# Start addresses of the large operands of a two-layer encoder moved to multiples of 64 bytes

## The chip, the cores and the metric

The kernel runs on one core of one Trainium2 chip. What is measured is the device time of one execution in microseconds (us), and the median of several runs is compared. Within the core, TensorE multiplies matrices (PE in the profile; PEld is its loading of the stationary operand), VectorE (DVE) and ScalarE (ACT) work elementwise, GpSimd (POOL) does small extra work, and SyncE (SP) issues most transfers. The operands of all of them lie in an on-chip memory of 128 partitions. A tile takes the same range of bytes in every partition, so that its place is one number: the byte in a partition at which it starts.

## The reference

The reference is an encoder of two layers over 256 tokens with 2048 channels, all in float32. Layer 0 mixes the tokens by gated linear attention in chunks, layer 1 by grouped attention with rotary positions. After each mixer stand an MLP with squared ReLU (2048 to 8192 to 2048) and a gated embedding:

```python
def reference(x, p, ...):
    h = x
    for i in range(DEPTH):                       # 2 layers
        u = rms_norm(h, g_pre_mix[i])
        mix = gla_mixer(u, ...) if i % 2 == 0 else gqa_mixer(u, ...)
        h = h + rms_norm(mix, g_post_mix[i])
        m = squared_relu_mlp(rms_norm(h, g_pre_mlp[i]), w_mlp_up[i], w_mlp_down[i])
        h = h + rms_norm(m, g_post_mlp[i])
        gate = sigmoid(h @ w_ple_gate[i])
        e = p[i] @ w_ple_proj[i]
        h = h + rms_norm(gate * e, g_ple[i])
    return h
```

Most of the arithmetic is products of a 256 x 2048 (or 256 x 8192) activation with weight matrices that are read once.

## The kernel before

Every large product is computed to nearly float32 accuracy from three products in the type float32r: an operand is split exactly into a high and a low part, and high x high, high x low and low x high are summed in one accumulator. The split activation lies in a tile `[128, 16, 512]` of 32 KiB in each partition: 16 contraction tiles of 128 rows, each with 256 columns of high and 256 columns of low part. There are two such tiles, `X` (the normalised residual) and `H` (what a mixer or the first half of the MLP has made).

The weights come through `WeightStream` (line 58), chunk by chunk in the order of use. A chunk is two contraction tiles of 512 columns, 4 KiB in a partition. It is loaded from memory into a `raw` buffer by SyncE (line 82), ACT writes its high part `whi` (line 91), and DVE writes its low part `wlo` (line 92). There are four buffers of each kind.

Two functions multiply:

- `gemm_b` (line 355) has the weights stationary and the activation moving. For each contraction tile and each 128 weight columns it issues a pair: `whi` against all 512 columns of `X` (line 367), then `wlo` against the 256 high columns (line 372). It makes q, k and og of layer 0 and, in four quarters per layer, the upward half of the MLP (u0 to u3; the page calls them all `u`).
- `gemm_a` (line 277) has the activation stationary and the weights moving, three products of 512 columns for each contraction tile and 128 rows (lines 294 to 296). With `X` stationary it makes v of layer 0, the keys, values and queries of layer 1 (kp, vp, q) and the gates (g); with `H` stationary the outputs of the mixers (go, ao) and the downward half of the MLP (d0 to d3).

`gemm_out` (line 301) is `gemm_a` for go, ao, d3 and g. Its last 512 columns are taken one row tile after the other (lines 333 to 335), and the first half of their weights waits in whichever of `X` and `H` is free: `X` for go, ao and d3, `H` for g. So there the moving operand is first one of the two large tiles and then a weight buffer, over the same stationary tile. The first row tile is multiplied 512 columns wide (48 matmuls), the second in two halves of 256.

The page names the moving operand first: `d<-whi,H` is `whi` moving over stationary `H`, `u<-X,whi` is `X` moving over stationary `whi`. The order of PE is the order in which the program is written; DVE and ACT are ordered by a scheduler.

Tiles get their addresses in the order in which pools and tiles are opened: first `ident`, `cols`, `mhalf` and `ones`, then `h` and `X`, then the weight buffers, then the pool `sm` of small tiles, the pool `mem` (tags `m2` and `e4`), and last what is opened for a while: the pool of the linear attention (`core`), or `L1` with `H` as its first tile. Each tile takes a multiple of 32 bytes.

Of the kernel before, what the change touches and what calls it, by code (L numbers as in the profile page):

```python
# [10 lines left out]
F32 = mybir.dt.float32  # L11
# [6 lines left out]
P = 128  # L18
# [17 lines left out]
NCOL = 84  # L36
# [19 lines left out]


class WeightStream:
    """Weight chunks in the order of use: DMA in, split exactly into two float32r parts."""

    def __init__(self, nc, pool, nraw, nsplit):
        self.nc, self.pool, self.nraw, self.nsplit = nc, pool, nraw, nsplit
# [29 lines left out]
        self.todo.append(lambda: self.nc.vector.tensor_sub(lo, raw, hi.bitcast(F32)))  # L92

    def parts(self, i):
        """The first chunk comes one contraction tile at a time, so that PE starts early."""
        kt = self.chunks[i][1]
        return [(k, k + 1) for k in range(kt)] if i == 0 else [(0, kt)]

# [52 lines left out]
def kernel(ctx, tc, a, out):  # L151
    nc = tc.nc
    base = ctx.enter_context(tc.tile_pool(name="base", bufs=1))
# [7 lines left out]
    def acc(name):  # L161
        return psa.tile([P, 512], F32, tag="acc", name=name)
# [60 lines left out]

    ident = base.tile([P, P], F32, name="ident")
    make_identity(nc, ident)
    cols = base.tile([P, NCOL], F32, name="cols")
    mhalf = base.tile([P, 8], F32, name="mhalf")
    nc.gpsimd.memset(mhalf, -0.5)
    ones = base.tile([P, 1], F32, name="ones")
    nc.gpsimd.memset(ones, 1.0)  # L230
    h = base.tile([P, NT, D], F32, name="h")
    X = base.tile([P, KT, 512], F32R, name="X")
# [41 lines left out]
    def region_open():  # L274
        region.enter_context(tc.manual_schedule(engines={mybir.EngineType.Activation, mybir.EngineType.DVE}))

    def gemm_a(op, ngroups, evac, nk=16, name="a", pair=False):
        nch = nk // KC
        order = [(g, c) for g in range(ngroups) for c in range(nch)]
        if pair:  # L280
            order = pair_order(nch) + [(g, c) for g in range(2, ngroups) for c in range(nch)]
        ps = {}
        for g, c in order:
            if c == 0:
                ps[g] = [acc(f"{name}_{g}_{t}") for t in range(NT)]
            hi, lo = W.get()
            seq = [(k, t) for k in range(KC) for t in range(NT)]
            if c == nch - 1:
                seq = [(k, t) for t in range(NT) for k in range(KC)]
            for k, t in seq:  # L290
                K = c * KC + k
                xh = op[:, K, t * P:(t + 1) * P]
                xl = op[:, K, T + t * P:T + (t + 1) * P]
                mm(ps[g][t], xh, hi[:, k], start=K == 0, stop=False)  # L294
                mm(ps[g][t], xh, lo[:, k], start=False, stop=False)  # L295
                mm(ps[g][t], xl, hi[:, k], start=False, stop=K == nk - 1)  # L296
                if K == nk - 1:
                    evac(g, t, ps[g][t])
            yield (g, c)

    def gemm_out(op, keep, evac, name, pair=False):
        """Four column groups; the last one row tile after the other, half of its weights waiting in `keep`."""
        nch = KT // KC
        p0 = W.pos + 3 * nch
        for c in range(NSPLIT):
            W.dest[p0 + c] = [keep[:, 4 * c + 2 * z:4 * c + 2 * z + 2].rearrange("p k n -> p (k n)") for z in range(2)]
        yield from gemm_a(op, 3, evac, name=name, pair=pair)
        for t in range(NT):
            parts = [(0, 512)] if t == 0 else [(0, 256), (256, 256)]
            ps = [acc(f"{name}_3_{t}_{o}") for o, _ in parts]  # L310
            order = [[c] for c in range(nch)]
            if t:
                order = order[NSPLIT:] + order[:NSPLIT]
                order[-2:] = [order[-2] + order[-1]]
            for n, cs in enumerate(order):
                end = n == len(order) - 1
                if t and end:
                    region_open()
                wt = {}
                for c in cs:  # L320
                    W.ahead()
                    wt[c] = W.pop(p0 + c) if t else W.split[p0 + c]
                if t and end:
                    W.pos += nch
                for (o, w), p_ in zip(parts, ps):
                    s = slice(o, o + w)
                    ck = [(c, k) for c in cs for k in range(KC)]
                    for c, k in ck:
                        K = c * KC + k
                        hi, lo = wt[c]  # L330
                        xh = op[:, K, t * P:(t + 1) * P]
                        xl = op[:, K, T + t * P:T + (t + 1) * P]
                        mm(p_[:, :w], xh, hi[:, k, s], start=n == 0 and k == 0, stop=False)
                        mm(p_[:, :w], xh, lo[:, k, s], start=False, stop=False)
                        mm(p_[:, :w], xl, hi[:, k, s], start=False, stop=end and (c, k) == ck[-1])
                    if end:
                        evac(3, t, p_[:, :w], o, w)
                yield (3, cs[0])
# [8 lines left out]
        return r  # L347

    def early(m, ss, name):
        """The update of the residual's first rows, while PE is at the second."""  # L350
        r = rstd_of(ss[:, :1, :4], D, name)
        for n in range(4):
            residual_n(m, r, n, (0,))
# [42 lines left out]
    def at(plan, slot, *fs):  # L396
        plan.setdefault(slot, []).extend(fs)
# [40 lines left out]
                                           op0=ALU.mult, op1=ALU.add)  # L438

    def boundary(m, ss, gain0, name, fill=(), late=None):  # L440
        """The normalised update of the residual and the next operand; fill: products that keep PE busy."""
        rstd = last_rstd(ss, name)
        mults = list(pend)
        pend.clear()
        W.ahead(1, lows=False)
        for f in fill[:-1]:
            f()()
        for o in (0, 256):
            nc.vector.scalar_tensor_tensor(h[:, 1, o:o + 256], m(1, 0)[:, o:o + 256], rstd, h[:, 1, o:o + 256],
                                           op0=ALU.mult, op1=ALU.add)  # L450
        W.lows()
        make_X(0, gain0)
        if late is not None:
            late(0)
        if fill:
            fill[-1]()()
        residual_n(m, rstd, 1, (1,))
        W.ahead(1)

        def hook(n):  # L460
            def f():
                make_X(n, gain0)
                if n == 2:
                    for g in mults:
                        g()
                if n < 3:
                    residual_n(m, rstd, n + 1, (1,))
                if late is not None:
                    late(n)
                if n == 3:  # L470
                    region.close()
            return f
        hooks = {0: [hook(1)], 2: [hook(2)], 4: [hook(3)]}
        if late is not None:
            at(hooks, 6, lambda: late(4))
        return hooks
# [137 lines left out]
    with tc.tile_pool(name="core", bufs=1) as cp:  # L614
# [150 lines left out]
        s = fold(ps, "lr", 32)  # L765
# [35 lines left out]
        sl = drive(gemm_a(X, 4, v_evac, name="v"), plan, sl)  # L801

    L1 = ctx.enter_context(tc.tile_pool(name="L1", bufs=1))
    H = L1.tile([P, KT, 512], F32R, name="H")

    def load_PT(i):
        pts = L1.tile([P, 2, T], F32, tag="pts", name=f"pts{i}")
        nc.scalar.dma_start(pts, a["pT"][i])
        PT = L1.tile([P, 2, 512], F32R, tag="PT", name=f"PT{i}")
        split_into(PT[:, :, :T], PT[:, :, T:], pts)  # L810
        return PT

    def og_evac(i, ps):
        s = fold(ps, f"og{i}")
        t1 = L1.tile([P, T], F32, tag="t1", name=f"og1_{i}", bufs=2)
        nc.vector.tensor_mul(t1, s, R0["r"])
        sg = L1.tile([P, T], F32, tag="t2", name=f"og2_{i}", bufs=2)
        nc.scalar.activation(sg, t1, AF.Sigmoid)
        nc.vector.tensor_mul(t1, t1, on[i // 4][:, i % 4])
        nc.vector.tensor_mul(t1, t1, sg)  # L820
        split_into(H[:, i, :T], H[:, i, T:], t1)
    drive(gemm_b(X, 4, og_evac, name="og"), plan, sl)
# [3 lines left out]
    mg = {}  # L826
    gr = gain_row(L1, a["g_post_mix"][0], "gpm0")
    ss = sm.tile([P, NT, 5], F32, tag="ss", name="ssm0")
    drive(gemm_out(H, X, out_evac(mg, gr, ss, "go"), "go"))

    RM = {}
# [13 lines left out]
    def mlp_ple(i, hooks, PT):  # L845
# [5 lines left out]
        def up_evac(f, ps):  # L851
# [3 lines left out]
            nc.scalar.activation(s2, s, AF.Square)  # L855
            split_into(H[:, f, :T], H[:, f, T:], s2)

# [16 lines left out]
        for q in range(4):  # L874
# [3 lines left out]
            if q < 3:  # L878
                drive(gemm_a(H, 4, down_evac(q), name=f"d{q}"))
            else:  # L880
                drive(gemm_out(H, X, down_evac(q), f"d{q}"))
        hooks = boundary(lambda t, n: macc[t][n], ss, None, f"rpl{i}", eprojs(e, range(EU[0] if i == 0 else EU[2], 8), PT))
        gr2 = {}

# [22 lines left out]
        def upd(t, n):  # L907
            return e[n][:, t]
        drive(gemm_out(X, H, gate_evac, f"g{i}"), hooks)
        return upd, ss2  # L910

# [265 lines left out]
```

## Time and profile before

| | before |
|---|---|
| median of 3 runs | 2332.02 us (2331.41 to 2332.15) |
| span of the profiled execution, first to last instruction | 2329.9 us |
| what lies around the span, median less span | 2.1 us |
| matmuls on PE | 11924 |
| PE busy | 2305.6 us, 99% |
| DVE, ACT busy | 1423.1 us (61%), 1213.8 us (52%) |
[...]

The profiled execution is known by its span alone; a run's time is 2.1 us longer than that span by the median. Matmuls overlap in the profile: each is shown from its own start to the modelled end of its pipeline, so that the next one starts while it is still shown. A busy share of 99% therefore tells that PE never waited long. It does not tell at what pace it went. The pace of a stage is read from the starts of its matmuls: the time from the start of one to the start of another, divided by how many lie between. [...] In a table by windows, the count in brackets is the number of matmuls shown in the window, and windows of the same length can be compared by it.

### The profile page before, as it was taken

How to read it: one execution, taken by the hardware profiler on the slowest of the kernel's cores; microseconds unless marked ns; L12 is line 12 of the kernel's file. 1: busy time of each engine (PE TensorE's matmuls, PEld its weight loads, DVE VectorE, ACT ScalarE, POOL GpSimd, SP SyncE). 2: the span in 40 equal slices, each digit the busy share in tenths (PEclk: the TensorE clock that was granted, in tenths of full speed). 3: DMA queues.
4: the chain of work that ended last, by engine and by line, in shares of the span. 5: the costliest groups of instructions: out<-in, count | busy, mean ns of one | idle time of the engine just before them, and what ended most of it. 6: DMA issues, size and time to landing. Idle time of an engine off the chain costs nothing.

```text
span 2329.9 us, 31200 instructions
## 1 busy us (share of the span) xinstructions
PE 2305.6 (99%) x11924; PEld 1955.4 (84%) x11924; DVE 1423.1 (61%) x1920; ACT 1213.8 (52%) x1884; POOL 36.7 (2%) x58
## 2 busy tenths in 40 slices
PE   8989999999999999999999999999999999999998
PEld 7878888988888888888888888888888888888887
DVE  6787765664564565556667676665455455455565
ACT  6666554654453454454456565555454355355454
POOL 0000000000000000000000010000000000000000
PEclk9999999999999999999999999999999999999999
DMA  8544665665665665665565644565565566566654
GB/s 285 158 145 144 203 187 189 192 188 189 189 190 186 187 188 186 188 191 187 194 216 160 181 137 158 200 190 189 186 187 189 187 189 189 187 187 188 210 171 145
DMA packets 223784, 431.75 MB, mean 185 GB/s; under 512 B 15697, under 2 KB 16721, under 8 KB 222865
## 3 DMA queue, kind: packets, MB, share of 16 engines
q1 hardware_dynamic: 221328, 421.23, 58.7%
q10 hardware_dynamic: 2304, 8.52, 1.0%
q8 instruction: 93, 1.52, 0.3%
q14 instruction: 59, 0.48, 0.1%
HBM read 427.60 MB, written 2.10 MB: 184 GB/s over the span
## 4 chain that ended last, share of the span: by engine, by line
PE 96%; DVE 1%; ACT 1%; issue 1%; DMA 0%; POOL 0%; SPq 0%; DVEq 0%; POOLq 0%; ACTq 0%
PE u L367 20%; PE u L372 10%; PE d L296 10%; PE d L294 10%; PE d L295 10%; PE og L367 3%; PE g L295 2%; PE g L294 2%; PE g L296 2%; PE og L372 1%; PE q L294 1%; PE q L296 1%; PE q L295 1%; PE k L367 1%; PE go L296 1%; PE ao L295 1%
## 5 line engine op out<-in xcount | busy, mean ns | idle before, releaser
L92 DVE TENSOR_TENSOR wlo<-raw,whi 128x1024 fp32r<-128x1024 f32 (+1 forms) x770 | 937.6, 1221 | 751.4 <-ACT whi L91 749.1
L91 ACT CAST whi<-raw 128x1024 fp32r<-128x1024 f32 (+1 forms) x770 | 805.5, 1049 | 875.3 <-PE d L296 357.3
L367 PE MATMUL u<-X,whi 128*128 128x512 f32 x2048 | 716.7, 395 | 0.0
L372 PE MATMUL u<-X,wlo 128*128 128x256 f32 x2048 | 572.1, 280 | 0.0
L367 PEld LDWEIGHTS u<-X,whi 128*128 128x128 f32 x2048 | 383.8, 187 | 89.5
L372 PEld LDWEIGHTS u<-X,wlo 128*128 128x128 f32 x2048 | 386.1, 189 | 0.4
L296 PE MATMUL d<-whi,H 128*128 128x512 f32 x960 | 380.6, 396 | 0.0
L294 PE MATMUL d<-whi,H 128*128 128x512 f32 x960 | 379.7, 395 | 0.0
L295 PE MATMUL d<-wlo,H 128*128 128x512 f32 x960 | 377.3, 393 | 0.0
L295 PEld LDWEIGHTS d<-wlo,H 128*128 128x128 f32 x960 | 180.2, 188 | 44.5
L296 PEld LDWEIGHTS d<-whi,H 128*128 128x128 f32 x960 | 180.2, 188 | 43.9
L294 PEld LDWEIGHTS d<-whi,H 128*128 128x128 f32 x960 | 180.2, 188 | 42.5
L367 PE MATMUL og<-X,whi 128*128 128x512 f32 x256 | 89.4, 393 | 0.0
L294 PE MATMUL g<-whi,X 128*128 128x512 f32 x192 | 75.2, 392 | 0.0
L295 PE MATMUL g<-wlo,X 128*128 128x512 f32 x192 | 74.7, 389 | 0.0
L296 PE MATMUL g<-whi,X 128*128 128x512 f32 x192 | 74.7, 389 | 0.0
L372 PE MATMUL og<-X,wlo 128*128 128x256 f32 x256 | 71.7, 280 | 0.0
L367 PEld LDWEIGHTS og<-X,whi 128*128 128x128 f32 x256 | 47.9, 187 | 10.5
L409 ACT COPY u_c<-u 128x256 f32<-128x256 f32 x128 | 47.1, 368 | 17.1 <-PE u L372 17.1
L367 PE MATMUL q<-X,whi 128*128 128x512 f32 x128 | 46.2, 411 | 6.1 <-ACT whi L91 5.3
L295 PE MATMUL v<-wlo,X 128*128 128x512 f32 x128 | 50.7, 396 | 0.8 <-DVE wlo L92 0.8
L294 PE MATMUL v<-whi,X 128*128 128x512 f32 x128 | 51.5, 402 | 0.0
(426 smaller groups left out, 2978.4 us busy)
## 6 DMA issues: line engine op xcount, KB each, us to landing
raw<-in_w_mlp_up SPq DMA_DIRECT2D x256, 512.0 KB, 3.7
raw<-in_w_mlp_down SPq DMA_DIRECT2D x256, 512.0 KB, 3.8
raw<-in_gla_w_in SPq DMA_DIRECT2D x95, 512.0 KB, 4.0
raw<-in_w_ple_gate SPq DMA_DIRECT2D x64, 512.0 KB, 4.2
raw<-in_attn_w_in SPq DMA_DIRECT2D x48, 512.0 KB, 4.2
raw<-in_gla_w_out SPq DMA_DIRECT2D x32, 512.0 KB, 4.3
raw<-in_attn_w_out SPq DMA_DIRECT2D x32, 512.0 KB, 4.3
raw<-in_w_ple_proj SPq DMA_DIRECT2D x7, 512.0 KB, 5.2
```

Source lines behind the costliest of these rows:

```text
L91: self.nc.scalar.copy(hi, raw)
L92: self.todo.append(lambda: self.nc.vector.tensor_sub(lo, raw, hi.bitcast(F32)))
L294: mm(ps[g][t], xh, hi[:, k], start=K == 0, stop=False)
L295: mm(ps[g][t], xh, lo[:, k], start=False, stop=False)
L296: mm(ps[g][t], xl, hi[:, k], start=False, stop=K == nk - 1)
L367: mm(ps[f], hi[:, k, f * P:(f + 1) * P], op[:, K, :], start=K == 0, stop=K == 15, skip_group_check=True)
L372: mm(ps[f][:, T:], lo[:, k, f * P:(f + 1) * P], op[:, K, :T], start=False, stop=K == 15, skip_group_check=True)
L409: nc.scalar.copy(cr[:parts], ps[:parts, T:])
```

## The change

Three small tiles at the start are made larger, and an unused tile of 32 bytes is put before `H`. The kernel uses the same parts of the enlarged tiles as before. Four docstrings and a class docstring become blank lines, and from the new tile on the lines are one higher.

```diff
-    cols = base.tile([P, NCOL], F32, name="cols")
-    mhalf = base.tile([P, 8], F32, name="mhalf")
+    cols = base.tile([P, 96], F32, name="cols")[:, :NCOL]
+    mhalf = base.tile([P, 16], F32, name="mhalf")[:, :8]
     nc.gpsimd.memset(mhalf, -0.5)
-    ones = base.tile([P, 1], F32, name="ones")
+    ones = base.tile([P, 16], F32, name="ones")[:, :1]
     nc.gpsimd.memset(ones, 1.0)
     h = base.tile([P, NT, D], F32, name="h")
     X = base.tile([P, KT, 512], F32R, name="X")
...
     L1 = ctx.enter_context(tc.tile_pool(name="L1", bufs=1))
+    L1.tile([P, 8], F32, name="gap")
     H = L1.tile([P, KT, 512], F32R, name="H")
```

On every engine the instructions are the same and stand in the same order. What moves is where the tiles start. Below is the first byte of each in a partition, by the built programs, and its remainder by 64. All offsets of the large operands within their tiles are multiples of 512 bytes, so the remainder of the tile is that of the operand.

| tile | before | remainder | after | remainder |
|---|---|---|---|---|
| h | 17440 | 32 | 17536 | 0 |
| X | 33824 | 32 | 33920 | 0 |
| raw (first of four) | 66592 | 32 | 66688 | 0 |
| whi (first of four) | 82976 | 32 | 83072 | 0 |
| wlo (first of four) | 99360 | 32 | 99456 | 0 |
| m2 tiles (first of eight) | 135104 | 0 | 135200 | 32 |
| e4 tiles (first of five) | 151488 | 0 | 151584 | 32 |
| H | 171968 | 0 | 172096 | 0 |
| PT, and the low parts of k and v in layer 1 (in L1) | 210880, 214976 | 0 | 211008, 215104 | 0 |

`X`, `raw`, `whi` and `wlo` move by 96 bytes together, `H` by 128. In layer 0 the operands of the linear attention (v in m2, S in the pool core) go from remainder 0 to 32 together. In layer 1, q, k, v and the softmax in m2 and e4 go from 0 to 32, but the low parts of k and v stay at 0.

## Rows read from the trace of the kernel before

**Rows 1.** The page, parts 1 and 2: busy time by engine; granted clock.

```profile
PE 2305.6 (99%) x11924; PEld 1955.4 (84%) x11924; DVE 1423.1 (61%) x1920; ACT 1213.8 (52%) x1884; POOL 36.7 (2%) x58
...
PEclk9999999999999999999999999999999999999999
```

**Rows 2.** PE's longest wait: who, for whom, us in total, times, longest.

```profile
PE q L367 <- ACT whi L91: 5.3, 1, 5.3
```

**Rows 3.** Windows (us), PE alone: length, busy (matmuls), clock, DMA share, GB/s.

```profile
260.00:320.00 60.00, 60.00 (x348) 1.00 0.64 191
620.00:690.00 70.00, 70.00 (x406) 1.00 0.64 190
700.00:770.00 70.00, 70.00 (x302) 1.00 0.59 188
790.00:860.00 70.00, 70.00 (x397) 1.00 0.64 187
1170.00:1210.00 40.00, 40.00 (x178) 1.00 0.62 207
1700.00:1770.00 70.00, 70.00 (x397) 1.00 0.64 186
1880.00:1950.00 70.00, 70.00 (x406) 1.00 0.66 192
```

**Rows 4.** PE's timeline in d1 of layer 0: start, length shown (us), instruction.

```profile
709.70 0.40 PE L296 MATMUL d<-whi,H 128*128 128x512 f32 x1
...
712.50 0.40 PE L296 MATMUL d<-whi,H 128*128 128x512 f32 x1
```

**Rows 5.** The same in the gate of layer 0.

```profile
1179.80 0.39 PE L296 MATMUL g<-whi,X 128*128 128x512 f32 x1
...
1182.52 0.39 PE L296 MATMUL g<-whi,X 128*128 128x512 f32 x1
```

**Rows 6.** The same at the end of layer 1's gate, from `H` to `whi`.

```profile
2298.71 0.40 PE L333 MATMUL g<-H,X 128*128 128x512 f32 x1
...
2304.56 0.39 PE L334 MATMUL g<-wlo,X 128*128 128x512 f32 x1
...
2306.60 0.39 PE L334 MATMUL g<-wlo,X 128*128 128x512 f32 x1
```

**Rows 7.** The page, part 5: two of the groups over stationary `H`, by line.

```profile
L294 PE MATMUL d<-whi,H 128*128 128x512 f32 x960 | 379.7, 395 | 0.0
...
L294 PE MATMUL go<-whi,H 128*128 128x512 f32 x96 | 37.6, 392 | 0.0
```

**Rows 8.** PE's timeline in u1 of layer 0.

```profile
629.68 0.39 PE L367 MATMUL u<-X,whi 128*128 128x512 f32 x1
...
631.76 0.39 PE L367 MATMUL u<-X,whi 128*128 128x512 f32 x1
```

**Rows 9.** PE's timeline in u2 of layer 0.

```profile
799.70 0.40 PE L367 MATMUL u<-X,whi 128*128 128x512 f32 x1
...
803.94 0.40 PE L367 MATMUL u<-X,whi 128*128 128x512 f32 x1
```

**Rows 10.** PE's timeline at the end of layer 0's gate, 256 columns wide.

```profile
1227.72 0.28 PE L334 MATMUL g<-wlo,X 128*128 128x256 f32 x1
...
1230.84 0.28 PE L333 MATMUL g<-H,X 128*128 128x256 f32 x1
...
1236.12 0.28 PE L333 MATMUL g<-H,X 128*128 128x256 f32 x1
```

**Rows 11.** PE's timeline in the linear attention, 256 columns wide.

```profile
175.35 0.28 PE L732 MATMUL o<-Sh,v 128*128 128x256 f32 x1
...
176.54 0.28 PE L733 MATMUL o<-Sl,v 128*128 128x256 f32 x1
```

**Rows 12.** The page, part 5: the split of the weights on DVE and ACT.

```profile
L92 DVE TENSOR_TENSOR wlo<-raw,whi 128x1024 fp32r<-128x1024 f32 (+1 forms) x770 | 937.6, 1221 | 751.4 <-ACT whi L91 749.1
L91 ACT CAST whi<-raw 128x1024 fp32r<-128x1024 f32 (+1 forms) x770 | 805.5, 1049 | 875.3 <-PE d L296 357.3
```

## The prediction, made before the changed kernel was run

> **What bounds the kernel now.** I read the page's busy times first, then PE's waits, then the starts of its matmuls stage by stage. PE is shown busy for 99% of the span at full clock, and DVE and ACT for 61% and 52% [rows 1]. Its longest wait is 5.3 us, once [rows 2]. So almost all of the 2329.9 us is the pace of PE, and a change that moves no instruction can matter only if it changes that pace.
>
> The pace is not the same everywhere, and that is the finding on which all rests. In the downward MLP (stationary `H`) 12 matmuls of 512 columns take 712.50 - 709.70 = 2.80 us, 233.3 ns each [rows 4]. In the gate (stationary `X`), the same lines with the same weight buffers moving, 12 take 2.72 us, 226.7 ns each [rows 5]. PE waits for nothing in either: both windows are full [rows 3]. [...]
>
> Is that the stage or the operand? At the end of layer 1's gate the stationary tile stays `X`, and the moving operand goes from `H` to the weight buffers. The pace goes from 5.85 us / 25 = 234.0 ns to 2.04 us / 9 = 226.7 ns from the second matmul on [rows 6]. So it depends on the two operands together. `X`, `whi` and `wlo` lie at remainder 32 by 64, `H` at 0. I call a pair of operands alike if both have the same remainder, else unlike. Alike (32 and 32) goes at 226.7 ns; unlike goes at 233.3 (moving 32, stationary 0) and at 234.0 (moving 0, stationary 32).
>
> The pairs of `gemm_b` are alike, and they have two paces at the same addresses: in u1 of layer 0 a pair (512 and 256 columns) takes 2.08 us / 6 = 346.7 ns [rows 8], in u2 4.24 us / 12 = 353.3 ns [rows 9]. By counts u1 of layer 0 and u2 of layer 1 go at the fast pace (406 matmuls in 70 us) and u2 of layer 0 and u1 of layer 1 at the slow one (397); og, which follows v, goes at the fast one (348 in 60 us) [rows 3]. Of the eight upward quarters four are fast and four slow, in turn. A stage keeps the pace that it falls into, so it is the way of entering it that picks one.
>
> **The change part by part.** The enlarged tiles and the gap issue nothing and cost nothing. What they do is move addresses: every large operand gets remainder 0, so that all pairs of `gemm_a` and `gemm_b` are alike.
>
> Stationary `H`: d has 3 x 960 matmuls of 512 columns, go and ao 2 x 3 x 96 [rows 7], which is 3456; the first row tiles of the closings of go, ao and the two d3 add 4 x 48 = 192, and the `H`-moving halves of the two gates 2 x 24 = 48. Together 3696 unlike matmuls. If alike at 0 costs what alike at 32 costs, each saves 233.3 - 226.7 = 6.67 ns: 3696 x 6.67 = **24.6 us**, all of it on the path that sets the end, since PE is that path throughout.
>
> Stationary `X` (v, kp, vp, q, the gates; 1536 + 48 matmuls): alike before and after, 0.
>
> The pairs of `gemm_b` (2560, of which 2048 in the upward quarters, 256 in each): alike before and after. Four quarters are slow: 4 x 256 x 6.67 = 6.8 us can be won if all become fast, or lost if all become slow. All slow quarters are entered from a stage with stationary `H`, which is unlike; og is entered from v, which is alike, and is fast [rows 3]. After the change all are entered from an alike stage, so og is the nearest row, and I take **6.8 us** won. Bounds: 6.8 won to 6.8 lost.
>
> Matmuls of 256 columns outside the pairs are about a thousand: 120.0 ns alike at 32 and 117.3 unlike (the first and the second stretch of [rows 10]), about 119.0 alike at 0 [rows 11]. Some of them become unlike or alike at 32 (layer 1's attention). With 1.0 ns or less between either and the middle, times some thousand, I set 0, bounds 2.7 us either way.
>
> Cover: at 226.7 ns a chunk of 12 matmuls lasts 2.72 us. Its split takes 1.05 us on ACT and 1.22 us on DVE [rows 12], so both have over half of it in hand, and the gate already runs full at this pace with its transfers at 207 GB/s [rows 3]. Nothing new becomes late. Elementwise tiles that go from 0 to 32 join `raw`, `whi` and `wlo`, which are worked on at 32 now; none of this work is what PE waits for, so I set it at 0.
>
> Sum: 2332.0 - 24.6 - 6.8 = **2300.6 us**. I count from the median, which is the profiled span of 2329.9 and 2.1 us around it; the change leaves these 2.1 alone. If the upward quarters fall the other way it is 2332.0 - 24.6 + 6.8 = 2314.2.
>
> [...]
>
> **The rivals.**
>
> *Remainder 0 is itself the dear one* (slower). Each unlike pair holds an operand at 0; it could be that operand that costs, whichever it is, and not the difference. Then `H` stays at 233.3 and the rest joins it: 1584 matmuls over `X` x 6.67 = 10.6 us, and the pairs either all lock into the slow pace (the 1536 fast ones x 6.67 = 10.2 us; 2352.8) or pay 6.67 ns in each of their two matmuls, 360.0 ns a pair (1536 x 13.3 + 1024 x 6.67 = 27.3 us; 2369.9). For it: both kinds of unlike pair cost nearly the same [rows 4, 6]. Against it: with both operands at 0, 256 columns take 119.0 ns, not more than the 120.0 of both at 32 [rows 10, 11]. It decides from 2.4 ns on: if alike at 0 costs x more than alike at 32, the stages with `H` gain 3696 x (6.67 - x) and the 1584 + 5120 others lose x each, even at x = 24.6 us / 10400.
>
> *The remainder by 64 is not what counts* (no change). `H` differs from the other tiles in more than that: by 128 it lies 64 - 32 = 32 off them before and 64 off after, and it is the only large tile far up in the partition. If a longer period or the distance counts, `H` stays unlike at 233.3 ns, `X` and the weights stay alike since they move together, and the time is 2332, give or take the 6.8 us of the upward quarters. For it: no row shows 512 columns with both at 0. Against it: that the two unlike orders cost the same fits a plain match of remainders as well. [...]
>
> *A start at 0 is cheaper for every moving operand* (much faster). With stationary `X`, 256 columns take 117.3 ns when `H` moves and 120.0 when `whi` moves [rows 10], 2.7 ns less from 0. If that holds beside the match, 7856 matmuls of 512 and the 2560 small halves of the pairs gain it: 10416 x 2.7 = 28 us, and the time is 2273. Against it: at 512 columns the moving `H` is dear, not cheap [rows 6].
>
> [...]
>
> **How the numbers follow.** The match of remainders: 0.46, at 2300.6, own range 2297 to 2317. No change: 0.24, at 2332. Remainder 0 dear: 0.22, from 2343 (the pairs untouched) to 2370. Cheaper everywhere: 0.08, at 2273. A measurement of this kernel can tell about 0.2%, 4.7 us, from no change. Faster: 0.46 + 0.08 = 0.54, of no change a little falls outside on either side (0.02 each), so faster 0.55, same 0.21, slower 0.24. The range leaves out the rival below and the dearer half of the one above: 2296 to 2353.
>
> **What would show it.** Right: in d the starts come 226.7 ns apart and a window of 70 us shows some 310 matmuls, not 302; the gate keeps 226.7; the end of the gate shows no step from `H` to `whi`; all upward quarters have 406 in 70 us. Wrong: d at 233.3 with all else as before (no change); the gate at 233 (remainder 0 dear); any stage over 512 columns below 226.7 (cheaper everywhere). If PE shows new waits for `wlo` or `whi`, the cover was misjudged.

## The result, and the profile after

The changed kernel takes **2316.43 us** (median; 2315.63 to 2318.29), against 2332.09 us of the kernel before beside it: a ratio of 0.9931 (interval 0.9917 to 0.9945), 15.7 us less. The forecast was 2300.6 us. The sign was right, the size about twice too large.

The page and PE's longest wait after (columns as in [rows 1, 2]):

```profile
PE 2290.0 (99%) x11924; PEld 1952.7 (84%) x11924; DVE 1422.7 (61%) x1920; ACT 1213.7 (52%) x1884; POOL 36.6 (2%) x58
```

```profile
PE q L367 <- ACT whi L91: 5.4, 2, 5.2
```

PE is as full as before, the other engines worked as long, no wait of PE changed by more than 0.2 us, and the mean granted clock was 0.997 of full speed, before 0.998. So all of the difference is pace. The windows of PE alone, placed in the stages of [rows 3]:

```profile
260.00:320.00 60.00, 60.00 (x349) 1.00 0.65 190
620.00:670.00 50.00, 50.00 (x290) 1.00 0.66 189
700.00:770.00 70.00, 70.00 (x307) 1.00 0.60 193
790.00:860.00 70.00, 70.00 (x398) 1.00 0.64 187
970.00:1040.00 70.00, 70.00 (x399) 1.00 0.64 187
1160.00:1200.00 40.00, 40.00 (x178) 1.00 0.60 201
1870.00:1940.00 70.00, 70.00 (x398) 1.00 0.64 186
```

Two things are to be read. d1 (700 to 770) went from 302 matmuls to 307, not to the 310 that the forecast wanted. And of the upward quarters u1 is at the fast pace (290 in 50 us are 406 in 70), but u2 and u3 are slow: 398 and 399 in layer 0 and, in the last row, 398 in u2 of layer 1, which was fast before with 406 [rows 3]. Over all eight quarters four were slow before (u0 and u2 of layer 0, u1 and u3 of layer 1), and six are after (u0, u2 and u3 of both). One execution of each kernel was profiled, so the quarters of the others are not seen.

PE's timeline in d1 and at the end of layer 1's gate gives the paces exactly (start, length shown, instruction):

```profile
704.82 0.39 PE L296 MATMUL d<-whi,H 128*128 128x512 f32 x1
...
732.29 0.39 PE L296 MATMUL d<-whi,H 128*128 128x512 f32 x1
```

```profile
2283.30 0.39 PE L333 MATMUL g<-H,X 128*128 128x512 f32 x1
...
2288.67 0.39 PE L335 MATMUL g<-H,X 128*128 128x512 f32 x1
...
2290.28 0.39 PE L333 MATMUL g<-whi,X 128*128 128x512 f32 x1
...
2291.64 0.39 PE L333 MATMUL g<-whi,X 128*128 128x512 f32 x1
```

The first two rows are 120 matmuls apart: 27.47 us / 120 = 228.9 ns, between the 233.3 of [rows 4] and the 226.7 of [rows 5]. At the gate's end `H` moving over `X` takes 5.37 us / 23 = 233.5 ns (234.0 before [rows 6]), and the weights moving over `X` 1.36 us / 6 = 226.7 from the seventh on, as before. So the step from `H` to `whi` that the forecast wanted gone is still there, though both operands now start at a multiple of 64.

Summed from the start of each matmul to the start of the next, by tile: the 512-column ones with `H` in them gave 16.0 us, those of 256 columns with `H` or `PT` in them 2.7; the upward quarters cost 2.6 more and the pairs of q and k 0.7. That is 15.4 of the 15.6 us by which the span fell (2329.9 to 2314.3).

### The profile page after: what moved, and what is told of

It is laid out like the page before. It is cut to its first block, busy times and chain, and to the rows that moved or that the text cites. A ratio compares the mean times of both kernels' runs of the same rounds, so it can differ in the third digit from the quotient of the medians.

```text
span 2314.3 us, 31200 instructions
## 1 busy us (share of the span) xinstructions
PE 2290.0 (99%) x11924; PEld 1952.7 (84%) x11924; DVE 1422.7 (61%) x1920; ACT 1213.7 (52%) x1884; POOL 36.6 (2%) x58
## 4 chain that ended last, share of the span: by engine, by line
PE 95%; DVE 2%; ACT 1%; issue 1%; POOL 0%; DMA 0%; SPq 0%; DVEq 0%; POOLq 0%; ACTq 0%
PE u L367 21%; PE u L372 10%; PE d L296 10%; PE d L295 10%; PE d L294 9%; PE og L367 3%; PE g L294 2%; PE g L296 2%; PE g L295 2%; PE og L372 1%; PE q L296 1%; PE q L295 1%; PE q L294 1%; PE k L367 1%; PE go L295 1%; PE ao L294 1%
## 5 line engine op out<-in xcount | busy, mean ns | idle before, releaser
L296 PE MATMUL d<-whi,H 128*128 128x512 f32 x960 | 376.2, 392 | 0.0
L294 PE MATMUL d<-whi,H 128*128 128x512 f32 x960 | 375.1, 391 | 0.0
```

## The experiments

**What of the move counts?** Four kernels took the change apart: the enlarged tiles without the gap, the gap without the enlarged tiles, and two with a gap of 96 bytes in place of 32. Two theories stood against each other: the remainder by 64 counts (a weight buffer that starts at a multiple of 64 helps), or the difference of the two operands' addresses, with a longer period.

*The enlarged tiles alone.* All large tiles but `H` at remainder 0, `H` at 172064, so at remainder 32.

```diff
-    L1.tile([P, 8], F32, name="gap")
```

> The three enlarged tiles alone, without the gap before H: X, raw, whi and wlo at remainder 0 by 64, H at 172064, remainder 32. The start of H less that of whi is 88992 bytes, as in the kernel before. Theory of the difference (the pace goes by how far the stationary operand lies from the moving one): d at 233.3 ns as before, the time 2332 us, give or take 7 us for the two paces of the pairs. Theory of the remainder (what helps is a weight buffer that starts at a multiple of 64): d at 229 ns, the time near 2316 us.

2332.3 us against 2333.33, ratio 0.9994 (0.9985 to 1.0004). The windows of d1 and u3:

```profile
700.00:770.00 70.00, 70.00 (x302) 1.00 0.59 189
970.00:1040.00 70.00, 70.00 (x405) 1.00 0.66 190
```

302 matmuls in d1: the pace of before. The four buffers that hold most operands now lie at multiples of 64, and nothing came of it. The distance from `whi` to `H` is 88992 bytes here, as before.

*The gap alone.* The small tiles as before, so that all large tiles are at remainder 32; `H` moves up by 32 bytes and nothing else of size moves.

```diff
     L1 = ctx.enter_context(tc.tile_pool(name="L1", bufs=1))
+    L1.tile([P, 8], F32, name="gap")
     H = L1.tile([P, KT, 512], F32R, name="H")
```

> The gap of 32 bytes before H alone, the small tiles as before: X, raw, whi and wlo at remainder 32 by 64, H at 172000, remainder 32 too. The start of H less that of whi is 89024 bytes, as in the changed kernel, but nothing large lies at a multiple of 64. Theory of the difference: d at 228.9 ns as in the changed kernel, the time 2316 us, give or take 7 us. Theory of the remainder: d at 233.3 ns, the time 2332 us.

2317.06 us, ratio 0.993 (0.9916 to 0.9945): the whole gain of the change. The windows of d1 and u2:

```profile
700.00:770.00 70.00, 70.00 (x307) 1.00 0.61 193
790.00:860.00 70.00, 70.00 (x397) 1.00 0.64 187
```

d1 has 307, exactly as the changed kernel. The distance from `whi` to `H` is 89024 bytes in both. No large tile is at a multiple of 64 here, so the property in the change's name does nothing; the 32 bytes in front of `H` are all of it. Nor is a plain match of remainders enough: `whi` and `H` are alike at 32, and go at 228.9 ns and not at the 226.7 of the alike `whi` and `X`.

*The change with `H` 64 bytes further up.* `H` at 172160, 89088 = 348 x 256 bytes above `whi`.

```diff
-    L1.tile([P, 8], F32, name="gap")
+    L1.tile([P, 24], F32, name="gap")
```

> The changed kernel with a gap of 96 bytes instead of 32: H at 172160, still a multiple of 64, and now a multiple of 1024 away from X, whi and wlo. Theory of the difference: d at 226.7 ns like the gate, 3648 matmuls x 2.2 ns = 8.1 us less than the changed kernel, 2308 us, give or take 7 us. Theory of the remainder by 64: nothing new, 2316 us.

2315.49 us, ratio 0.9923 (0.9908 to 0.9938). The windows of u1, d1, u2 and u3:

```profile
620.00:680.00 60.00, 60.00 (x342) 1.00 0.65 189
700.00:770.00 70.00, 70.00 (x311) 1.00 0.61 193
790.00:860.00 70.00, 70.00 (x398) 1.00 0.65 187
970.00:1040.00 70.00, 70.00 (x398) 1.00 0.64 186
```

d1 has 311: 226.7 ns, the forecast's pace, got not by the remainder by 64, which is 0 as in the changed kernel, but by 64 bytes more of distance. The time hardly fell against the changed kernel, and lies just outside the expected 2308, give or take 7, since by the starts in the trace all eight upward quarters are now slow (342 in 60 us are 399 in 70). Summed as above, the 512-column matmuls with `H` gave 23.8 of the forecast's 24.6 us, and the quarters took back 5.8, since four of them were slow before: 18.0 us less by these two, and 2333.33 - 2315.49 = 17.8 us less were measured.

*The kernel before with a gap of 96 bytes.* All large tiles at remainder 32, the distance again 89088.

```diff
+    L1.tile([P, 24], F32, name="gap")
```

> The kernel before with a gap of 96 bytes before H: X, raw, whi, wlo and H all at remainder 32 by 64, and H a multiple of 1024 away from the others. Theory of the difference: the same as the changed kernel with a gap of 96 bytes, d at 226.7 ns, 2308 us, give or take 7 us. Theory of the remainder: no operand at a multiple of 64, so no gain, 2332 us.

2316.23 us, ratio 0.9928 (0.9914 to 0.9943). The windows of d1 and u2:

```profile
700.00:770.00 70.00, 70.00 (x311) 1.00 0.61 194
790.00:860.00 70.00, 70.00 (x398) 1.00 0.64 187
```

The same paces as the run before this one, and again just outside the expected time for the same reason, with no large operand among `X`, `H` and the weights at a multiple of 64. What counts is the difference of the two addresses.

**The price of a difference.** A kernel of its own, nothing of the reference in it: 48 equal matmuls in a row for each setting, the stationary tile moved by steps of 32 bytes against the moving one.

```
    def run(st, s, m, cols=512, count=48):
        ...
        p = acc()
        for i in range(count):
            mm(p[:, :cols], st[:, s // 4:s // 4 + P], M[:, m // 4:m // 4 + cols], ...)
    ...
    for d in range(0, 1024, 32):
        run(S, d, 0)
```

> Not the encoder but a measurement of the disputed cost by itself: the input x is split off into float32r tiles M (moving) and S, U (stationary) that start a multiple of 1024 bytes apart, x is copied to the output, and nothing of the reference is computed. 48 matmuls of 512 columns each for S starting 0, 32, 64 ... 992 bytes further than M, then the same for starts of M at remainder 32 and 64, for 4, 8, 16 and 48 bytes, for U that lies 112 KiB up, then pairs of 512 and 256 columns, then 256 columns alone. Theory of the difference: the pace is a function of the start of S less that of M alone, with a period: 226.7 ns at 0, 233.3 at 160, 228.9 at 192, some 234 at 96, 233.3 at 64, as the stages showed; the same numbers for M at remainder 32 or 64 and for U. Theory of the remainder: it changes with the start of M and not with the difference. If distance far up in the partition counts, U differs from S.

PE's timeline, one row for the 48 matmuls of a setting (start, length shown, instruction, count); the differences are 0, 32, 64 and so on to 256:

```profile
24.70 11.05 PE L55 MATMUL tab<-M,S 128*128 128x512 f32 x48
35.59 11.35 PE L55 MATMUL tac<-M,S 128*128 128x512 f32 x48
46.78 11.36 PE L55 MATMUL tad<-M,S 128*128 128x512 f32 x48
57.98 11.40 PE L55 MATMUL tae<-M,S 128*128 128x512 f32 x48
69.22 11.32 PE L55 MATMUL taf<-M,S 128*128 128x512 f32 x48
80.38 11.37 PE L55 MATMUL tag<-M,S 128*128 128x512 f32 x48
91.58 11.16 PE L55 MATMUL tah<-M,S 128*128 128x512 f32 x48
102.58 11.36 PE L55 MATMUL tai<-M,S 128*128 128x512 f32 x48
113.77 0.61 PE L55 MATMUL taj<-M,S 128*128 128x512 f32 x2
```

From row to row: 10.89 us at difference 0 (226.9 ns each), 11.00 at 192 (229.2), 11.16 to 11.24 at all others (232.5 to 234.2). Without the first matmuls of each setting, and over whole repeats of the pattern of its starts:

| start of stationary less start of moving, bytes by 256 | 0 | 32 | 64 | 96 | 128 | 160 | 192 | 224 |
|---|---|---|---|---|---|---|---|---|
| ns, 512 columns | 226.7 | 233.3 | 233.3 | 234.3 | 232.4 | 233.3 | 228.9 | 233.3 |
| ns, 256 columns | 120.0 | 118.3 | 117.8 | 117.3 | 118.7 | 120.0 | 117.8 | 117.8 |

The row for 512 columns repeats every 256 bytes up to 992, and is the same with the moving operand 32 or 64 bytes on and with the stationary one in a tile 112 KiB up. So neither address matters alone, nor the distance in full. The table holds the paces of the plain 512-column products in the kernels, to within 0.3 ns:

| operands (stationary, moving) | difference before | pace | after | pace |
|---|---|---|---|---|
| `H`, `whi` and `wlo` | 160 | 233.3 | 192 | 228.9 |
| `X`, `H` (end of the gate) | 96 | 234.0 | 64 | 233.5 |
| `X`, `whi` and `wlo` | 0 | 226.7 | 0 | 226.7 |

The same kernel ran pairs as `gemm_b` has them, both weights at one difference from the moving tile. Differences 0, 32 and 64 gave 353.3 ns, 96 and 224 gave 346.7, the rest between.

**Pairs with two differences.** Is there a faster place for `whi` and `wlo` under `X`? All 8 x 8 differences of the two, nothing else computed.

> The same tiles; nothing of the reference is computed and x is copied to the output. Pairs as in gemm_b, 24 for each of 64 settings: the stationary tile of the 512 columns starts 0, 32 ... 224 bytes further than a multiple of 1024 from the moving one, that of the 256 columns likewise, with 12 matmuls of a like pair ahead of each. If the two paces of a pair (346.7 and 353.3 ns) come from the way of entering it alone, no setting is always at 346.7; if they come from the differences, as in gemm_a, some settings lie at 346.7 or below and others at 353.3 or above, and the weight buffers can be placed so that all upward quarters are fast.

Most lie from 346.7 to 353.3 ns. The lowest is 340.0, at (64, 0) and (192, 0), the high weights' difference first. At (0, 0), where the kernel's pairs lie, it is 353.3.

**What the other products would pay.** Moving `whi` for that would move it against `X` and `H` in `gemm_a` too, whose 512-column products go in threes (high, low, high weights over one stationary tile). All 8 x 8 differences of the two weights, and the best pairs entered in five ways.

> Again tiles alone; nothing of the reference is computed and x is copied to the output. Triples as in gemm_a (high weights, low weights, high weights moving over the stationary tile) for 64 settings: the stationary tile 0, 32 ... 224 bytes further than the high weights, and likewise than the low ones. Then pairs with the high weights 64, 192 and 96 bytes and the low ones 0, 0 and 32 bytes further than the moving tile, each entered in five ways (13 to 15 matmuls of another difference ahead). If each matmul has the price of its own difference, a triple at 0 and 0 takes 680 ns, at 192 and 0 2 x 228.9 + 226.7 = 684.5 ns, and none less than 680; if prices depend on the difference of the matmul before, as the pairs showed (340.0 ns at 64 and 0, below any sum), some triples are below 680. If the pace of a pair is set by the differences, the five ways of entering give one number for each of the three settings, 340.0, 340.0 and 343.3 to 346.7 ns; if by the entry, they scatter.

A triple takes 680.0 ns at (0, 0), that is 3 x 226.7, and no other place is below 686.6. (192, 0) takes 700 and not the 684.5 that the table's prices add up to: what a matmul costs depends on its neighbours too. In `gemm_a` the roles of `whi` and `X` are exchanged, so the difference changes its sign: with `whi` at (64, 0) for its pairs the triples over `X` lie at (192, 0), and an estimate for the 1584 matmuls over `X` alone is 1584 x 6.67 = 10.6 us more. With `whi` at (192, 0) they lie at (64, 0), where a triple takes 702.7 ns, and it is 1584 x 7.6 = 12.0 us. And the 340 isn't sure: (64, 0) gave 340, 340, 350, 353.3 and 350 by the five entries, (192, 0) 340, 350, 350, 340 and 350, and the third place tried, (96, 32), 343.3, 352, 343.3, 352 and 343.3. The place of the weights was left as it is. By these runs the differences set which paces a stream of pairs can have, and the entry picks one.

**Which entry picks the fast pace?** Pairs at difference 0 after 16 to 18 plain matmuls at difference 0 or 192 (five entries), and the first pair taken in 15 ways: whole, cut into narrower pieces, or with an extra small half ahead of it; nothing of the reference is computed.

> Tiles alone again; nothing of the reference is computed and x is copied to the output. Pairs with all operands at difference 0, as in gemm_b after every version that brings H to a like place, entered in 75 ways: 16 to 18 matmuls at difference 0 or 192 ahead, and then the first pair whole, or cut into pieces of other widths (256 and 256, 128 and 384, 64 and 448 and so on), or a small half first. If a stage keeps the pace that its entry picks, each way gives 346.7 or 353.3 ns to the end, and a cut that costs nothing brings the fast one; if the addresses alone set it, all 75 give one number. Whole pairs after difference 0 gave 353.3 before, and should again.

PE's timeline after 16 plain matmuls, first with whole pairs, then with the first small half in two pieces of 128 columns (start, length shown, instruction, count):

```profile
20.53 0.39 PE L59 MATMUL tab<-M,S 128*128 128x512 f32 x1
20.76 0.28 PE L60 MATMUL tab<-M,S 128*128 128x256 f32 x1
20.87 0.40 PE L59 MATMUL tab<-M,S 128*128 128x512 f32 x1
...
22.99 0.40 PE L59 MATMUL tab<-M,S 128*128 128x512 f32 x1
...
28.29 0.40 PE L59 MATMUL tab<-M,S 128*128 128x512 f32 x1
```

```profile
120.02 0.39 PE L79 MATMUL taj<-M,S 128*128 128x512 f32 x1
120.25 0.33 PE L83 MATMUL taj<-M,S 128*128 128x128 f32 x2
120.42 0.45 PE L59 MATMUL taj<-M,S 128*128 128x512 f32 x1
...
123.24 0.40 PE L59 MATMUL taj<-M,S 128*128 128x512 f32 x1
...
128.45 0.39 PE L59 MATMUL taj<-M,S 128*128 128x512 f32 x1
```

From 22.99 to 28.29 are 15 pairs, 353.3 ns each; from 123.24 to 128.45 also 15, 347.3 by the rounded starts and 346.67 over the last 12. Same addresses, same instructions from the second pair on, and each stream kept its pace to the end. Whole pairs were slow by all five entries. The cut small half was fast by four of five, the pieces (448, 64) and (192, 320) of the first large half by four each, (128, 384) by none. An extra small half in two pieces ahead of whole pairs was fast by all five. I found no rule in which cuts do it. The settings also differ in the accumulator that they write, but in the kernel the pairs of one quarter write four of them in turn and keep one pace.

**The cut in the kernel.** `H` at the difference 0 (the run with the gap of 96 bytes above), and the first small half of u1, u2 and u3 in two pieces; in u0, which goes on from an earlier part, that of its second group.

```diff
-                def low(k, f):
+                def low(k, f, w=T):
...
+                        for o in range(0, T, w):
+                            mm(ps[f][:, T + o:T + o + w], ..., op[:, K, o:o + w], ...)
...
-                        low(k, f)
+                        low(k, f, 128 if name[0] == "u" and n == 0 and c == 0 and g == fresh else T)
```

> The changed kernel with a gap of 96 bytes (H a multiple of 1024 away), and in each upward quarter of the MLP one matmul of 256 columns over the low weights cut in two of 128: in the first pair of u1, u2 and u3, and in u0 at the start of its second group, after the elementwise work that enters it. If the entry alone picks the pace of like pairs, all eight quarters go at 346.7 ns instead of 353.3: 8 x 256 x 6.67 = 13.7 us less, 0.1 us back for each cut, so 2302 to 2303 us. If the cut does not reach the fast pace after d, nothing changes: 2315.5 us.

**2306.2 us** (2305.98 to 2306.95) against 2332.67, ratio 0.9884 (0.987 to 0.9899): below both kernels of the study, and 3 us above what was expected. The windows of u1, d1 and u3:

```profile
610.00:680.00 70.00, 70.00 (x407) 1.00 0.66 190
700.00:770.00 70.00, 70.00 (x310) 1.00 0.62 195
960.00:1030.00 70.00, 70.00 (x406) 1.00 0.67 190
```

u1 to u3 are fast in both layers. By the starts each takes 88.85 us where it took 90.44 in the run without the cut, so 6 x 1.59 = 9.5 us less; by the medians of the two runs 9.3 came. u0 stayed slow in both layers (353.3 ns a pair): there the cut comes eight pairs after other products, and it did not lead to the fast pace. With 192 pairs at stake in each u0 that is 2 x 192 x 6.67 ns = 2.6 us that didn't come.

*A cut at the start of every group of 64 pairs.* The same with `g >= fresh`.

> The same with the cut in the first pair of each group of 512 weight columns, four in a quarter (three in u0). If a cut always leads to the fast pace, 2303 to 2305 us; if it picks a new pace each time, some groups are slow again and the time lies between 2303 and 2316 us.

2310.82 us, ratio 0.9903 (0.9886 to 0.9919). Two windows in the first two groups of u1:

```profile
603.00:618.00 15.00, 15.00 (x88) 1.00 0.69 200
625.00:640.00 15.00, 15.00 (x86) 1.00 0.68 200
```

and the cut between them, at the start of the second group:

```profile
616.09 0.39 PE L367 MATMUL u<-X,whi 128*128 128x512 f32 x1
...
620.25 0.39 PE L367 MATMUL u<-X,whi 128*128 128x512 f32 x1
620.48 0.33 PE L373 MATMUL u<-X,wlo 128*128 128x128 f32 x2
620.65 0.45 PE L367 MATMUL u<-X,whi 128*128 128x512 f32 x1
...
623.17 0.40 PE L367 MATMUL u<-X,whi 128*128 128x512 f32 x1
...
626.00 0.40 PE L367 MATMUL u<-X,whi 128*128 128x512 f32 x1
```

Ahead of the cut a pair takes 4.16 us / 12 = 346.7 ns; after it 2.83 us / 8 = 353.8. In u1 to u3 the four groups go fast, slow, fast, slow; in u0 the cut freed the third group, and the fourth stayed fast. So a cut isn't a cure of its own: in a stream that is already fast it mostly costs the fast pace. One at the entry paid (2306.2 us), one in each group gave back half of it (2310.82 us).

## Why the prediction was right or wrong

**What bounds it.** Right: no instruction moved, no wait of note came or went, and the time followed the pace of PE's matmuls.

**The match of remainders, 24.6 us.** This is the step that failed. It took from two differing pairs that equal remainders by 64 make a pair alike. The remainder by 64 was only what the rows then at hand could not tell from the real property: the difference of the two starts by 256. The move took it from 160 to 192, and 192 is by the table the second best of the eight, by chance neither alike nor unlike: 228.9 ns. The term is then 3648 matmuls over `H` x 4.44 = 16.2 us, by the matmuls' starts 16.0, and the 48 matmuls that move `H` stay where they were (233.5). The 6.67 ns that the prediction took are right for the difference 0, as the two runs with 96 bytes of gap showed. [Rows 6] had a hint: 234.0 for the one unlike pair and 233.3 for the other, which I read as equal; they are the table's 96 and 160.

**The upward quarters, 6.8 us.** Wrong in sign: 2.6 us lost. That the way of entering picks the pace was right, but the argument for the fast one, that the slow quarters follow an unlike stage and og, which is fast, an alike one, was not. u1 of layer 0 and u2 of layer 1, which were fast [rows 3], follow the same unlike stages. After plain matmuls at difference 0 whole pairs were slow by every entry tried, in the kernel and by themselves; og's first 64 pairs are broken up by other products, and go at 353 to 354 ns from the second pair on in the two pieces of 16 and at 347 in the one of 32 between them, before it stays at 346.7, so it was no model of an entry from a steady stage. By quarters: u3 of layer 0 and u2 of layer 1 became slow (2 x 1.7 us), u0 of layer 1 for its last 192 pairs (1.3), u1 of layer 1 became fast (-1.7), and the first groups of u0 gave back 0.4. Which pace a quarter takes is not set by the differences between `X`, `H` and the weights alone: with the enlarged tiles alone they were as before, yet u0 of layer 1 was slow (353.3 ns a pair, 346.7 before), and u1 to u3 of that layer each had the other pace than before.

**256 columns, set at 0.** 2.7 us less, at the edge of the bound. The 117.3 ns of [rows 10] were not the price of every unlike pair: over `H`, unlike too, 256 columns took 120.0 before, as the table has it at 160. After, at 192, they take 117.8 in go and ao, again as the table has it, but 113.3 in d3 (start, length shown, instruction):

```profile
401.07 0.28 PE L333 MATMUL go<-whi,H 128*128 128x256 f32 x1
...
405.55 0.28 PE L335 MATMUL go<-whi,H 128*128 128x256 f32 x1
```

```profile
1121.81 0.28 PE L333 MATMUL d<-whi,H 128*128 128x256 f32 x1
...
1126.80 0.28 PE L335 MATMUL d<-whi,H 128*128 128x256 f32 x1
```

That is 4.48 us for 38 matmuls and 4.99 us for 44, over the same tiles, so 117.9 and 113.4 ns by the rounded starts. So streams of 256 columns too can have two paces at one place, and the lower one lies below the whole table. What picks it here was not tried.

**Cover, elementwise work, the gate over `X`: 0.** Right: the gate's window shows 178 matmuls in 40 us as before, and no wait for `wlo` or `whi` grew by more than 0.1 us.

**The rivals.** *Remainder 0 is dear* fell with the enlarged tiles alone, 0.9994. *The remainder by 64 is not what counts* was right in what it said of the property, a longer period, and wrong that `H` would stay at 233.3 by it; it took every other difference for equally dear. The 32 bytes in front of `H` alone, with no large tile at a multiple of 64, took 16.3 us off (2333.33 to 2317.06). *Cheaper everywhere*: no stage of plain 512-column matmuls is below 226.7 in any run.

**The sum, and luck.** With the terms as measured it is 2332.0 - 16.0 - 2.7 + 2.6 + 0.7 = 2316.6 us, and 2316.43 were measured. That the time fell, and by about half of the forecast, was luck: by the table a move of `H` to any other difference but 0 would have left its stages between 232.4 and 234.3 ns, no more than 1 ns from where they were.

**What stays open.** What in the chip makes the difference by 256 count, and what decides which pace pairs, or products of 256 columns, fall into. The runs show the table and the entries, not their cause.

## What to carry to other kernels

Where PE is full, read the pace from the starts and compare stages that differ in one operand: a few ns a matmul were 1% of this kernel (23.8 of 2333.33 us for the 512-column ones with `H` at the difference 0). Before naming the property of an address that sets it, measure that property by itself over its whole range; two rows fit too many periods. And place a tile by its difference to the partner that it meets most often, then look again at the streams whose pace depends on how they are entered, since they can take some of the gain back (5.8 of those 23.8 us).

## What was not expected of the hardware

- 512-column matmuls of float32r with a weight load each took from 226.7 to 234.3 ns in the measurement of the price, at a granted clock of 1.0, by (start of stationary - start of moving) modulo 256 bytes, and by neither start alone. Steps below 32 bytes counted as well: 232.4 at 4 bytes, 230.6 at 8, 233.3 at 16 and 48.
- Matmuls of 256 columns followed another order: 120.0 ns at 0 and 160, 117.3 at 96. At 192 they took 117.8 in go and ao of the changed kernel and 113.3 in d3.
- A stream of a 512- and a 256-column matmul at one place, the difference 0, had two lasting paces, 346.7 and 353.3 ns, and in u1 to u3 a single matmul cut in two at its start, with nothing else changed, set the pace of the 256 pairs of the quarter.
- Prices didn't add: three matmuls at the differences 192, 0, 192 took 700 ns, where the single ones sum to 684.5.
